# Second FFN of a two-FFN encoder layer: one low part moved from VectorE to an accumulating DMA, the first pair's preparation one block later, and the first half's output scaling one block later

## The chip, the cores and the metric

One NeuronCore of a Trainium2 chip. The metric is the device time in microseconds (us). Before the change it is 821.62 us, the median of three runs (821.60 to 821.70).

## The reference

One layer of an encoder on 512 positions of width 1024, in float32:

```python
x = x + 0.5 * swiglu(rms_norm(x, ffn1_norm), ffn1_w_gate, ffn1_w_up, ffn1_w_down)
h = rms_norm(x, mix_norm); u = h @ w_in
x = x + jnp.concatenate([fourier_mixer(...), gqa_attention(...)], axis=-1) @ w_out
x = x + 0.5 * swiglu(rms_norm(x, ffn2_norm), ffn2_w_gate, ffn2_w_up, ffn2_w_down)
return rms_norm(x, final_norm)
# swiglu(h, g, u, d) = (silu(h @ g) * (h @ u)) @ d ; hidden width 2752
```

## The kernel before, in words

Everything is kept transposed: `x[k]` (tile `gx`) holds 128 of the 1024 features by 512 positions. A float32 product is made of two rounded parts: a **high part** (a cast or copy on ScalarE, ACT below) and a **low part**, source minus high part (`lows`, L128, a subtraction on VectorE, DVE). Each 128x128 block of weights then takes three matmuls on TensorE (PE): high by high, high by low, low by high (`product`, L184). A low part can also be made without DVE: `rest_by_dma` (L157 and L158) lets ACT write minus the high part, and an accumulating DMA from GpSimd's queue (POOL) then adds the source to it.

The layer runs in three stages: the first FFN (`ffn`, tiles with 0 in the name of the norm), the mixer (a list of names sets the order), and the second FFN (`ffn` again, `n_` is 2; "stage 2" below). `ffn` treats the hidden width as 21 chunks of 128 and a tail "t" of 64 columns, in four groups. In stage 2 the groups are (0, t, 1), 2 to 7, 8 to 13 and 14 to 20.

- The first three plain chunks (0, 1, 2) and the tail are multiplied directly (`gate`, PSUM tiles `gu`), 24 matmuls of 512 columns for each 128 columns of gate or up. Meanwhile `operands` (L329) prepares the right-hand sides for the rest: for i = 0 to 3, a block `b_i` (x times gain times 1/rms, L337, 128x512 twice), four differences `t_i` (L344), the high parts (L347) of three quarters of `b_i` and of all of `t_i`, and their low parts. The low part of `t_i` (128x1024) is always DVE's; that of `b_i` (128x768) is DVE's for i = 0 and 1 and a DMA's for i = 2 and 3.
- All other chunks are made in pairs of gate and up by a scheme with seven products instead of eight (`seven`, L420, PSUM tiles `r`, `p`, `q`). Their weights come from `prepare`: two loads of 512 KB on SP's queue (`raw_g` and `raw_u`, L371), sums and differences (`s`, L394), casts (L379, L388) and low parts (L128). The steps of `prepare` are handed out one by one, between the blocks of what runs at that time.
- After each group, `down` multiplies the group's chunks by the down weights, for d = 0 to 7 (PSUM tiles `dn`, loads `raw_dn` at L152, cast at L170, low at L128), and `residual` (L544, DVE) adds the result to `x[d]`. For the first group of stage 2 a block d has 8 matmuls: 3 for chunk 0, 2 for the tail (L502, L503), 3 for chunk 1. In its order the first low weight part is used by the third matmul.

`raw_u`, `raw_dn` and the direct weights share three load buffers (tag `raw`); `raw_g` and the `b_i` share two (tag `raw_g`). A load therefore waits until an earlier user of its buffer has been read for the last time. In stage 2 the first pair is chunk 3: `prepare(3)` is called at block d = 1 of the first group's `down`, in stage 1 at d = 2.

PE and SP run in the written order. The order on ACT, DVE and POOL is chosen when the program is built, by a scheduler that knows the dependences; each engine then runs its own list in order.

The end (`closing`): for the last group, d = 5 to 7 are made by features for positions 0 to 255 and by tokens for positions 256 to 511, 128 positions at a time (c = 2 and c = 3, `by_tokens`, L534: 7 steps i = 0 to 6 of three matmuls). Between these steps stand the sums for 1/rms of the first half, `finish_half` (L1314: two transposes, L261, put the row of 1/rms into PSUM; ACT copies it to `rb`, L269; DVE scales six blocks in three instructions, L1327; POOL scales two, L1322; and each result is stored), and `finish` for c = 2 inside c = 3's steps (another L261, which needs 1/rms of c = 2). That 1/rms is made after c = 2's last matmul by a square with a sum on ACT (L1356), an addition on DVE (L1366) and a power on POOL (L1367). c = 3 goes through the same three instructions, and then through L1387 and L1391 to the last stores.

Of the kernel before, what the change touches and what calls it, by code (L numbers as in the profile page):

```python
# [86 lines left out]
def encoder(ctx, tc, A, out):  # L87
# [19 lines left out]
    def bank(name):  # L107
        return pp.tile([P, S], F32, tag="bank", name=name)
# [18 lines left out]
    def lows(lo, src, hi):  # L127
        nc.vector.tensor_tensor(out=lo, in0=src, in1=asf(hi), op=ALU.subtract)  # L128
# [26 lines left out]
    def rest_by_dma(lo, hi, src):  # L155

        nc.scalar.activation(lo, asf(hi), AF.Copy, scale=-1.0)  # L157
        nc.gpsimd.dma_start(out=lo, in_=src, accum_op=ALU.add)  # L158
# [123 lines left out]
    def ffn(norm, after, wgu, wd, wdt, groups, opening, closing):  # L282
# [4 lines left out]
        n_ = norm.n  # L287
        n_plain = len(groups[0])
        with tc.tile_pool(name=f"act{n_}", bufs=1) as ap, tc.tile_pool(name=f"sums{n_}", bufs=2) as sp:
# [7 lines left out]
            def place(j):  # L297
                where[j] = free.pop(0)
                return where[j]
# [8 lines left out]
            def gate(c, between={}, by_dma=False):  # L308
                whi, wlo = weights(wgu[c], f"gu{n_}_{c}", by_dma=by_dma)
                ps = bank(f"gu{n_}_{c}")  # L310
                for k in range(KD):
                    between.get(k, int)()
                    product(ps, whi[:, k, :], wlo[:, k, :], hh[k], hl[k], k == 0, k == KD - 1, turn=True)
                return ps

            def tail_weights():

                raw = wp.tile([P, D], F32, tag="raw", name=f"rawt{n_}")
                nc.sync.dma_start(out=raw[0:FT], in_=wdt)
                nc.sync.dma_start(out=raw[FT:P], in_=wdt)  # L320
                thi = slot()
                plain.insert(0, plain.pop())
                nc.scalar.copy(thi, raw)
                for i in range(2):
                    c = slice(i * S, (i + 1) * S)
                    wt.append(tp.tile([P, S], F32R, tag="sq", name=f"wt{n_}_{i}"))
                    nc.scalar.copy(wt[i][0:FT], asf(thi[0:FT, c]))
                    lows(wt[i][FT:P], raw[FT:P, c], thi[FT:P, c])
# [4 lines left out]
            def operands(rp, i0, i1):  # L333
                for i in range(i0, i1):
                    b = sp.tile([P, 4, HALF], F32, tag="raw_g", name=f"b{n_}_{i}")
                    for o, k in ((0, i), (2, i + KH)):
                        nc.vector.scalar_tensor_tensor(  # L337
                            out=b[:, o : o + 2].rearrange("p a b -> p (a b)"), in0=x[k],
                            scalar=gains[:, norm.n, k : k + 1], in1=rp, op0=ALU.mult, op1=ALU.mult,
                        )  # L340
                    b12, b11, b22, b21 = (b[:, o] for o in range(4))
                    t = sp.tile([P, 4, HALF], F32, tag=("s12", "s34")[i % 2], bufs=1, name=f"t{n_}_{i}")
                    for o, (p, q) in enumerate(((b12, b11), (b22, t[:, 0]), (b22, b12), (b21, t[:, 1]))):
                        nc.vector.tensor_tensor(out=t[:, o], in0=p, in1=q, op=ALU.subtract)  # L344
                    for src, c in ((b[:, 1:], slice(0, 3)), (t, slice(3, 7))):
                        h, l = rt[:, c, 0, i], rt[:, c, 1, i]
                        nc.scalar.copy(h, src)  # L347
                        if src is t or i < 2:
                            lows(l, src, h)
                        else:  # L350
                            rest_by_dma(l, h, src)

            def back(ts):
                plain[:] = [t for t in plain if all(t is not q for q in ts)]
# [188 lines left out]
            def residual(d, ps, t):  # L543
                nc.vector.scalar_tensor_tensor(  # L544
                    out=x[d][:, t], in0=ps[:, t], scalar=0.5, in1=x[d][:, t], op0=ALU.mult, op1=ALU.add
                )

            every = slice(0, S)
            for gi, group in enumerate(groups):
                last = gi == len(groups) - 1  # L550
                ahead = []
                if gi:
                    rest = seven(range(group[0] + 1, min(group[-1] + 2, NF)), ready)
                else:
                    lent = [acts[:, FRONT + i * KD * P : FRONT + (i + 1) * KD * P] for i in range(PLACES - 4, PLACES)]
                    plain.extend(lent)
                    row = []
                    pss = dict(enumerate(opening(gate, lambda: norm.column([norm.acc]), lambda: row.append(norm.row()))))
                    back(lent[:2])
                    due, parts, left = [*pss, "t"], list(range(KH)), range(2 * len(pss), 2 * n_plain)  # L560
                    pss["t"] = [gate(2 * NF)]
                    tail_weights()
                    for i, c in enumerate(left):
                        pss.setdefault(c // 2, []).append(gate(c, by_dma=i in (1,) if n_ else i > 0))
                        if due:
                            j = due.pop(0)
                            evacuate(at[:, place(j)], n_, pss[j], norm)
                        if c % 2 and c != left[-1]:
                            due.append(c // 2)
                        while len(parts) * len(left) > (len(left) - 1 - i) * KH:  # L570
                            o = parts.pop(0)
                            operands(row[0], o, o + 1)

                    def rest():
                        evacuate(at[:, place(n_plain - 1)], n_, pss[n_plain - 1], norm)

                def added(d, ps):
                    residual(d, ps, every)
                    if last:
                        (after.sums if closing else after.add)(d)  # L580
                    if ahead:
                        f, *a = ahead.pop(0)
                        f(*a)

                waiting, downs = [], []
                for d in range(KD):
                    if last and closing and d == KD - LAST:
                        closing(
                            [(e, down(e, group, gi)) for e in range(d, KD)], residual,
                            lambda ps, c: by_tokens(ps, c, group), finished,  # L590
                        )
                        break
                    if last and d == KD - 2:
                        back(lent)
                    ps = bank(f"dn{n_}_{d}_{gi}")
                    while len(downs) < min(d + 1 + (0 if gi or not n_ else 2), KD):
                        downs.append(down(len(downs), group, gi))
                    steps = downs[d](ps, every)
                    for _ in range(len(group) - (last and d < 2)):
                        next(steps)  # L600
                    waiting.append((d, ps, steps))
                    if d == (1 if gi or n_ else 2) and not last:
                        ready = prepare(groups[gi + 1][0] + 1)
                        ahead.extend(ready[1])
                    if d == 0:
                        rest()
                        if last:

                            lent = slots[KD - 2 : KD]
                            plain[2:2] = lent  # L610
                            continue
                    for d_, ps, steps in waiting:
                        for _ in steps:
                            pass
                        added(d_, ps)
                    waiting = []
                for f, *a in ahead:
                    f(*a)
                if not gi:
                    back(lent)  # L620
                free.extend(where[j] for j in group)
# [711 lines left out]
    def closing(downs, residual, by_tokens, finished):  # L1333
# [62 lines left out]
        for c in (2, 3):  # L1396
            ps = bank(f"last{c}")
            for i, _ in enumerate(by_tokens(ps, c)):
                if (c, i) == (2, 2):
                    n3.column([n3.acc], 0, 2)  # L1400
                    sums = bank("ss3_2")
                    n3.sum(sums, 2, [n3.acc])
                    n3.mean(sums, 2, 3)
                if (c, i) == (2, 5):
                    finish_half()
                if (c, i) == (3, 3):
                    finish(*done[-1])
            inverse(c, ps, z)
            done.append((c, ps))
# [126 lines left out]
```

## Time and profile before

| what | us |
|---|---|
| median of three runs | 821.62 |
| the profiled execution | 822.25 |
| its span, first to last instruction | 820.4 |
| outside of the span | 1.85 |
| direct products of stage 2 begin / its first `down` begins | 485.62 / 524.00 |
| first seven-product pair of stage 2 begins | 539.24 |
| last matmuls of c = 3 begin / span ends | 812.52 / 820.4 |

How to read it: times are from the span's start. PEld is PE's loading of the stationary operand, which runs ahead of the matmul that uses it. A row of the timeline has start, length, engine, line, operation, output<-inputs, shapes and count; in square brackets stands how long the engine had been idle and what ended that. Successive instructions overlap by about 0.1 us in these rows, so what one of them costs its engine is the distance from its start to the next one's start, a little less than its own length. Names leave buffer numbers out: which block a row belongs to follows from its place in the engine's order.

### The profile page before, as it was taken

Reading aid. Unit: us, or ns where it says so; the run is one execution under the profiler, and the core shown is the slowest. Engines: PE = TensorE matmul, PEld = TensorE weight load, DVE = VectorE, ACT = ScalarE, POOL = GpSimd, SP = SyncE. Lnnn points to the kernel's source line nnn. Section 1 sums busy time; section 2 is a strip of 40 time slices with the busy share of each in tenths; the row PEclk is TensorE's granted clock in tenths of the full one; section 3 lists DMA queues with packets and bytes.
Section 4 is the critical chain, followed back from the end, with each engine's and each line's share of the span. In section 5 each row is a group of like instructions: output and inputs, shape, how many; then the busy total and the mean of one; then the engine's idle time right before and its main releaser. Section 6 shows DMA issues by size and latency. Waiting matters only on the chain.

```text
span 820.4 us, 13609 instructions
## 1 busy us (share of the span) xinstructions
PE 813.2 (99%) x5362; PEld 745.9 (91%) x5362; DVE 638.9 (78%) x1004; ACT 482.4 (59%) x809; POOL 28.1 (3%) x30
## 2 busy tenths in 40 slices
PE   9999999999999999999999999999999999999997
PEld 7889999899989998889998888899989999899986
DVE  7898896479856847799998579998945896479574
ACT  7763674157523735699998458556632673257462
POOL 0110000000000000220000000100000000000001
PEclk9999999999999999999999999999999999999999
DMA  7664322323142213342101233552333322322222
GB/s 257 173 145 178 126 93 77 124 103 141 59 155 71 95 61 116 129 147 67 64 26 52 84 119 93 127 171 107 95 122 115 127 97 70 130 104 97 69 77 103
DMA packets 31168, 89.58 MB, mean 109 GB/s; under 512 B 3712, under 2 KB 8832, under 8 KB 31104
## 3 DMA queue, kind: packets, MB, share of 16 engines
q1 hardware_dynamic: 27776, 82.61, 29.3%
q0 software_dynamic: 2608, 5.12, 3.4%
q10 hardware_dynamic: 720, 0.98, 0.3%
q8 instruction: 42, 0.69, 0.3%
q14 instruction: 22, 0.18, 0.1%
HBM read 84.24 MB, written 2.10 MB: 105 GB/s over the span
## 4 chain that ended last, share of the span: by engine, by line
PE 93%; DVE 2%; ACT 1%; DMA 1%; issue 1%; POOL 0%; POOLq 0%; DVEq 0%; ACTq 0%
PE dn L184 25%; PE r L420 23%; PE q L420 12%; PE gu L184 7%; PE mix L184 6%; PE p L420 6%; PE gu L709 3%; PE mix L1203 2%; PE mix L1169 2%; PE mix L1007 1%; PE mix L1008 1%; PE mix L1009 1%; PE mix L1066 1%; PE mix L1143 1%; PE mix L1144 1%
## 5 line engine op out<-in xcount | busy, mean ns | idle before, releaser
L420 PE MATMUL r<-rt,ring 128*128 128x256 f32 x1686 | 209.2, 276 | 0.0
L184 PE MATMUL dn<-at,ring 128*128 128x512 f32 x900 | 203.3, 381 | 0.4 <-DVE ring L128 0.4
L420 PEld LDWEIGHTS r<-rt,ring 128*128 128x128 f32 x1686 | 200.3, 188 | 0.8
L184 PEld LDWEIGHTS dn<-at,ring 128*128 128x128 f32 x900 | 168.1, 188 | 29.8 <-DVE ring L128 1.5
L420 PE MATMUL q<-rt,ring 128*128 128x256 f32 x840 | 106.7, 276 | 0.0
L128 DVE TENSOR_TENSOR ring<-s,ring 128x1024 fp32r<-128x1024 f32 x70 | 85.7, 1224 | 24.0 <-ACT ring L379 20.6
L420 PEld LDWEIGHTS q<-rt,ring 128*128 128x128 f32 x840 | 100.4, 188 | 0.1
L544 DVE SCALAR_TENSOR_TENSOR gx<-dn,gx 128x512 f32<-128x512 f32 x61 | 42.0, 691 | 66.7 <-PE dn L184 66.7
L379 ACT CAST ring<-s 128x1024 fp32r<-128x1024 f32 x70 | 73.5, 1050 | 28.0 <-PE p L420 12.7
L170 ACT CAST ring<-raw_dn 128x768 fp32r<-128x768 f32 (+3 forms) x58 | 45.3, 784 | 70.8 <-PE dn L184 59.9
L128 DVE TENSOR_TENSOR ring<-raw_dn,ring 128x768 fp32r<-128x768 f32 (+3 forms) x58 | 51.6, 893 | 5.7 <-PE r L420 4.4
L420 PE MATMUL p<-rt,ring 128*128 128x256 f32 x420 | 53.3, 276 | 0.0
L128 DVE TENSOR_TENSOR ring<-raw_g,ring 128x1024 fp32r<-128x1024 f32 x35 | 42.8, 1222 | 11.1 <-PE p L420 10.2
L420 PEld LDWEIGHTS p<-rt,ring 128*128 128x128 f32 x420 | 50.2, 188 | 0.0
L184 PE MATMUL gu<-ring 128*128 128x512 f32 x216 | 48.9, 381 | 0.0
L379 ACT CAST ring<-raw_g 128x1024 fp32r<-128x1024 f32 x35 | 36.8, 1051 | 17.6 <-DMA raw_g<-in_wgu 11.9
L184 PEld LDWEIGHTS gu<-ring 128*128 128x128 f32 x216 | 40.4, 188 | 6.9
L428 ACT COPY p<-r 128x256 f32<-128x256 f32 x35 | 13.0, 371 | 46.7 <-PE r L420 46.3
L452 ACT ACTIVATE g<-g 128x512 f32<-128x512 f32 x35 | 22.1, 633 | 23.5 <-DVE g L451 23.3
L388 ACT CAST ring<-raw_u 128x512 fp32r<-128x512 f32 x35 | 21.8, 624 | 15.9 <-PE q L420 15.0
L465 DVE TENSOR_TENSOR u<-g,u 128x512 f32<-128x512 f32 x35 | 24.1, 690 | 6.1 <-ACT u L464 6.0
L184 PE MATMUL mix<-near,ring 128*128 128x512 f32 x120 | 28.8, 381 | 0.0
(266 smaller groups left out, 1314.5 us busy)
## 6 DMA issues: line engine op xcount, KB each, us to landing
raw_g<-in_wgu SPq DMA_DIRECT2D x35, 512.0 KB, 3.6
raw_u<-in_wgu SPq DMA_DIRECT2D x35, 512.0 KB, 4.4
raw_dn<-in_wd SPq DMA_DIRECT2D x40, 384.0 KB, 3.1
raw_gu<-in_wgu SPq DMA_DIRECT2D x12, 512.0 KB, 3.9
raw_o<-in_wo SPq DMA_DIRECT2D x8, 512.0 KB, 3.6
raw_dn<-in_wd SPq DMA_DIRECT2D x8, 448.0 KB, 3.5
raw_wq<-in_wins SPq DMA_DIRECT2D x4, 512.0 KB, 3.5
raw_f<-in_winf SPq DMA_DIRECT2D x4, 512.0 KB, 3.5
```

The lines of the kernel that those rows point to most:

```text
L128: nc.vector.tensor_tensor(out=lo, in0=src, in1=asf(hi), op=ALU.subtract)
L170: nc.scalar.copy(hi[:, :n, :], raw[:, :n, :])
L184: nc.tensor.matmul(ps, a, b, start=first and b is mhi and a is whi, stop=last and a is wlo)
L379: nc.scalar.copy(hi, src)
L388: nc.scalar.copy(hi, src)
L420: nc.tensor.matmul(ps[:, t], a[:, ks], b[:, i, t], start=first and i == 0 and o == 0, stop=i == KH - 1 and o == 2, skip_group_check=not first,
L452: nc.scalar.activation(b["g"], b["g"], AF.Silu)
L465: nc.vector.tensor_tensor(out=u, in0=b["g"], in1=u, op=ALU.mult)
L544: nc.vector.scalar_tensor_tensor(out=x[d][:, t], in0=ps[:, t], scalar=0.5, in1=x[d][:, t], op0=ALU.mult, op1=ALU.add)
L709: nc.tensor.matmul(turned(pss[c]), w[:, k % 2, c], turned(m[k]), start=k == 0 and m is hh and w is hi, stop=k == KD - 1 and w is lo,)
L1169: nc.tensor.transpose(pts[n][:, c * P : (c + 1) * P], prob[t, b, c][:, kc * P : (kc + 1) * P], ident)
L1203: nc.tensor.matmul(turned(outs[t, b]), w, turned(p), start=kc == 0 and i == 0, stop=kc == 3 and i == 1)
```

## The change

Three edits, in three places:

```diff
                     for src, c in ((b[:, 1:], slice(0, 3)), (t, slice(3, 7))):
                         h, l = rt[:, c, 0, i], rt[:, c, 1, i]
                         nc.scalar.copy(h, src)
-                        if src is t or i < 2:
+                        if src is t or i < (1 if n_ else 2):
                             lows(l, src, h)
                         else:
                             rest_by_dma(l, h, src)
...
                     waiting.append((d, ps, steps))
-                    if d == (1 if gi or n_ else 2) and not last:
+                    if d == (1 if gi else 2) and not last:
                         ready = prepare(groups[gi + 1][0] + 1)
                         ahead.extend(ready[1])
...
-                if (c, i) == (2, 5):
+                if (c, i) == (2, 6):
                     finish_half()
```

In stage 2 the low part of `b_1` is now made by ACT and a DMA, as those of `b_2` and `b_3` are. `prepare(3)` is called at d = 2. `finish_half` stands behind all seven steps of c = 2 instead of behind six.

What moves on the engines, as the built programs have it. First SP, at the loads of stage 2's first `down` and first pair (`raw_dn_3_0` is block d = 3 of group 0). Before:

```order
L152 DMA raw_dn_3_0_5340<-in_wd 128x256
L371 DMA raw_g_3_5352<-in_wgu 128x1024
L371 DMA raw_u_3_5353<-in_wgu 128x1024
L152 DMA raw_dn_4_0_5362<-in_wd 128x256
L152 DMA raw_dn_5_0_5377<-in_wd 128x256
```

and after the change:

```order
L152 DMA raw_dn_3_0_5341<-in_wd 128x256
L152 DMA raw_dn_4_0_5355<-in_wd 128x256
L371 DMA raw_g_3_5367<-in_wgu 128x1024
L371 DMA raw_u_3_5368<-in_wgu 128x1024
L152 DMA raw_dn_5_0_5377<-in_wd 128x256
```

The load for d = 4 now stands ahead of the pair's loads. With that the buffers change hands: by the waits in the programs, `raw_u_3` took the buffer of d = 1 and now takes that of d = 2; d = 5 took that of `raw_u_3` and now takes that of d = 3; d = 6 took that of d = 3 and now takes that of `raw_u_3`; d = 4 took that of d = 2 and now takes that of d = 1.

Second DVE, in the same stretch (`rt<-t_2` is a low part of `operands`, `ring<-raw_dn_3_0` the low part of block d = 3's weights, `gx<-dn_0_0` the residual of d = 0, `s_2_3` the sums of pair 3). Before:

```order
L128 TENSOR_TENSOR ring<-raw_dn_2_0_5318,ring 128x256
L128 TENSOR_TENSOR rt_5006<-t_2_5257,rt_5006 128x4x256
L128 TENSOR_TENSOR rt_5006<-t_3_5299,rt_5006 128x4x256
L629 TENSOR_TENSOR u2p<-gu_5_5271,rb_3385 128x512
L128 TENSOR_TENSOR ring<-raw_g_3_5352,ring 128x1024
L394 TENSOR_TENSOR s_2_3_5356<-raw_u_3_5353 128x512
L394 TENSOR_TENSOR s_2_3_5357<-raw_g_3_5352,raw_u_3_5353 128x512
L631 TENSOR_TENSOR u2p<-g2p,u2p 128x512
L128 TENSOR_TENSOR ring<-raw_u_3_5353,ring 128x512
L544 SCALAR_TENSOR_TENSOR gx<-dn_0_0_5309,gx 128x512
L128 TENSOR_TENSOR ring<-raw_dn_3_0_5340,ring 128x256
```

and after:

```order
L128 TENSOR_TENSOR rt_5006<-t_2_5258,rt_5006 128x4x256
L128 TENSOR_TENSOR rt_5006<-t_3_5300,rt_5006 128x4x256
L128 TENSOR_TENSOR ring<-raw_dn_2_0_5319,ring 128x256
L128 TENSOR_TENSOR ring<-raw_g_3_5367,ring 128x1024
L629 TENSOR_TENSOR u2p<-gu_5_5272,rb_3385 128x512
L631 TENSOR_TENSOR u2p<-g2p,u2p 128x512
L544 SCALAR_TENSOR_TENSOR gx<-dn_0_0_5310,gx 128x512
L128 TENSOR_TENSOR ring<-raw_dn_3_0_5341,ring 128x256
L394 TENSOR_TENSOR s_2_3_5371<-raw_u_3_5368 128x512
L394 TENSOR_TENSOR s_2_3_5372<-raw_g_3_5367,raw_u_3_5368 128x512
```

The three instructions on `raw_u_3` now stand behind the low part for d = 3, and that for d = 2 stands behind two long low parts of `operands`. Further down, the low part for d = 5 moves ahead of the last difference of pair 3 and that for d = 6 ahead of the long low part of its first sums, while one low part of 128x512 and one sum of 128x512 change places around d = 4.

Third POOL, from stage 2 to the end, as a difference (`r<-squares` is the power L1367 for c = 2 and c = 3, `gx<-gx,rb` the two scalings of `finish_half`):

```order
 L158 DMA ring<-in_wgu 128x1024
-L158 DMA rt_5006<-b_2_5254 128x3x256
-L158 DMA rt_5006<-b_3_5296 128x3x256
+L158 DMA rt_5006<-b_1_5205 128x3x256
+L158 DMA rt_5006<-b_2_5255 128x3x256
+L158 DMA rt_5006<-b_3_5297 128x3x256
 L256 TENSOR_TENSOR r_4993<-ms_4994,mhalf 128x2
+L1367 TENSOR_TENSOR r_4993<-squares,mhalf 128x1
 L1322 TENSOR_TENSOR gx<-gx,rb_4995 128x256 x2
-L1367 TENSOR_TENSOR r_4993<-squares,mhalf 128x1 x2
+L1367 TENSOR_TENSOR r_4993<-squares,mhalf 128x1
```

One more transfer is issued, and the power for c = 2 stands ahead of the two scalings. In the same way ACT's square for c = 2 (L1356) now stands ahead of the copy to `rb`, and DVE's addition (L1366) ahead of the three scalings (L1327). DVE's `b_3` (L337) now waits for `b_1`'s transfer too, since it takes that block's buffer.

## The prediction

> **What bounds the kernel now.** I read the page's busy times and its chain first, then who PE waited for, and then the places of the waits in the timeline.
>
> ```profile
> PE 813.2 (99%) x5362; PEld 745.9 (91%) x5362; DVE 638.9 (78%) x1004; ACT 482.4 (59%) x809; POOL 28.1 (3%) x30
> PE 93%; DVE 2%; ACT 1%; DMA 1%; issue 1%; POOL 0%; POOLq 0%; DVEq 0%; ACTq 0%
> PE dn L184 <- DVE ring L128: 0.4, 1, 0.4
> PE rp L261 <- POOL r L1367: 0.2, 1, 0.2
> ```
>
> PE is busy for 99% of the span and 93% of the chain is PE. The change takes no matmul away, so it can gain only what PE loses, and the two named waits of PE are exactly at the places that it touches: a low part of a down weight in stage 2, and POOL's power near the end. By these rows there would be 0.4 + 0.2 = 0.6 us to win. But matmul ends are modelled, so I take distances of starts instead.
>
> ```profile
> 524.00 0.82 PE L184 MATMUL dn<-at,ring 128*128 128x512 f32 x3
> 530.29 0.19 PEld L184 LDWEIGHTS dn<-at,ring 128*128 128x128 f32 x1 [0.82 <-DVE ring L128]
> 533.97 0.19 PEld L184 LDWEIGHTS dn<-at,ring 128*128 128x128 f32 x1 [0.27 <-DVE ring L128]
> 536.03 0.19 PEld L184 LDWEIGHTS dn<-at,ring 128*128 128x128 f32 x1 [0.44 <-DVE ring L128]
> 539.24 1.65 PE L420 MATMUL r<-rt,ring 128*128 128x256 f32 x13
> 600.62 27.72 PE dn L184 x126
> ```
>
> Undisturbed, a matmul of this kind costs 27.72 / 126 = 0.22 us (last row, a later group). The first `down` of stage 2 has 8 x 8 = 64 of them, 14.08 us, and took 539.24 - 524.00 = 15.24. So **1.16 us** are lost there, in three places: the weight loads for d = 3, 5 and 6 waited for DVE's low parts. At the end:
>
> ```profile
> 807.35 1.79 PE L534 MATMUL last<-ring,at 128*128 128x384 f32 x9
> 808.97 0.39 PE L261 MATMUL rp<-ident,r 128*128 128x128 f32 x2
> 809.95 2.25 PE L534 MATMUL last<-ring,at 128*128 128x384 f32 x12
> 812.44 0.32 PE L261 MATMUL rp<-ident,r 128*128 128x128 f32 x1 [0.24 <-POOL r L1367]
> ```
>
> Nine token matmuls take 808.97 - 807.35 = 1.62, 0.18 each; twelve from 809.95 end at 812.11, and the next instruction started at 812.44. **0.33 us** are lost.
>
> The Trainium skill ("Perfetto Trace Analysis", Identifying the Most-Contended Engine) judges PE by its weight loads, not by matmul occupancy. By the loads' idle times the first `down` would lose 0.82 + 0.27 + 0.44 = 1.53 us instead of 1.16, and the sum below would be 1.86. I keep the starts, since a load may wait while earlier matmuls still run.
>
> **The low part of `b_1`.**
>
> ```profile
> 503.51 0.96 DVE L128 TENSOR_TENSOR rt<-b,rt 128x768 fp32r<-128x768 f32 x1
> 504.38 0.42 DVE L344 TENSOR_TENSOR t<-b,t 128x256 f32<-128x256 f32 x1
> 511.02 1.40 DVE L337 SCALAR_TENSOR_TENSOR b<-gx,rp 128x512 f32<-128x512 f32 x2
> DVE ring L128 <- ACT ring L379: 0.5, 1, 0.5
> ```
>
> DVE loses one instruction worth 504.38 - 503.51 = 0.87 us. From 496 to the end of the first `down` its only wait over 0.2 us is the last row, for the cast of `raw_g`, so everything behind moves ahead by 0.87 until something else is late. ACT gets one copy (L157) of 0.84 us, and POOL one transfer:
>
> ```profile
> 502.86 1.05 ACT L170 CAST at<-raw_gu 128x1024 fp32r<-128x1024 f32 x1 [1.59 <-PE gu L184]
> 512.48 0.85 ACT L157 ACTIVATE rt<-rt 128x768 fp32r<-128x768 f32 x1
> 513.90 1.29 POOL L158 DMA_DIRECT2D rt<-b  x1 [12.12 <-ACT rt L157]
> DMA to landing us min/median/max: 4.8/5.4/6.4
> ```
>
> The copy falls into the 1.59 us in which ACT waited for PE; without that cover it would push the next cast by 0.84. POOL had been idle for 12.12 us. The new cost is a wait: `b_3` (511.02 before, 510.15 now) needs `b_1`'s buffer. The high part of `b_1` is what ACT did last before its 1.59 us of idling, so it ends at 502.86 - 1.59 = 501.27, and the copy at 502.1; with 4.8 to 6.4 us (all accumulating transfers of this kernel) it lands at 506.9 to 508.5, 1.6 us or more in time. Queued behind `b_3` on DVE are all low parts of the down weights, so this margin counts. I take nothing for it; the other end stands among the rivals. The transfer's landing at 508.5 is also 30 us ahead of the pair that reads it (539.24).
>
> The Trainium skill ("SBUF — State Buffer", the box on the "DVE blocks DMA" trap) speaks against this edit: a transfer issued from GpSimd can stand still while a DVE copy holds the port that they share; it gives 620 ns alone and 3100 ns beside one. With these 2.5 us more, an estimate by that page, the landing would be at 511.0 and DVE would lose its 0.87; the sum would fall to about 1.0. The trace does not agree: `b_2`'s transfer was issued in 1.29 us (513.90) in a stretch where DVE did not rest, though its work there is differences and no plain copies.
>
> **The pair one block later.** What moves behind, and what each low part then has as margin:
>
> ```profile
> 521.80 0.42 DVE L128 TENSOR_TENSOR ring<-raw_dn,ring 128x256 fp32r<-128x256 f32 x1
> 522.25 2.36 DVE L128 TENSOR_TENSOR rt<-t,rt 128x1024 fp32r<-128x1024 f32 x2
> 524.52 0.69 DVE L629 TENSOR_TENSOR u2p<-gu,rb 128x512 f32<-128x512 f32 x1
> 529.22 0.69 DVE L544 SCALAR_TENSOR_TENSOR gx<-dn,gx 128x512 f32<-128x512 f32 x1
> 529.82 0.42 DVE L128 TENSOR_TENSOR ring<-raw_dn,ring 128x256 fp32r<-128x256 f32 x1
> 531.36 0.42 DVE L128 TENSOR_TENSOR at<-raw_dn,at 128x256 fp32r<-128x256 f32 x1
> 533.49 0.42 DVE L128 TENSOR_TENSOR ring<-raw_dn,ring 128x256 fp32r<-128x256 f32 x1
> 535.56 0.42 DVE L128 TENSOR_TENSOR ring<-raw_dn,ring 128x256 fp32r<-128x256 f32 x1
> 536.49 0.42 DVE L128 TENSOR_TENSOR at<-raw_dn,at 128x256 fp32r<-128x256 f32 x1
> ```
>
> The five short ones from 529.82 on are d = 3 to 7. Undisturbed, block d starts at 524.00 + 1.76 d and uses its low part 0.44 later: 529.72, 531.48, 533.24, 535.00 and 536.76. The new starts are the old ones less 0.87, less what moves behind (0.60 for 128x512, by 529.82 - 529.22; 1.14 for 128x1024, half of the 2.27 between 522.25 and 524.52):
> - d = 3: three instructions on `raw_u` go behind it: 529.82 - 0.87 - 1.80 = 527.15, over 2 us in time.
> - d = 4: one goes ahead, one behind: 530.49, ends 530.91, 0.57 in time.
> - d = 5: 533.49 - 0.87 - 0.60 = 532.02, 0.80 in time.
> - d = 6: 535.56 - 0.87 - 1.14 = 533.55, 1.03 in time.
> - d = 7: the same set ahead: 535.62, 0.72 in time.
>
> A weight load has to go ahead of its matmul by about one matmul, 0.22, which leaves 0.35 at the tightest. So the 1.16 us go. What is late next is `raw_u`:
>
> ```profile
> 521.10 0.33 SPq L371 DMA_DIRECT2D raw_g<-in_wgu  x1
> 521.51 0.38 SPq L371 DMA_DIRECT2D raw_u<-in_wgu  x1
> raw_u<-in_wgu SPq DMA_DIRECT2D x35, 512.0 KB, 4.4
> raw_g<-in_wgu SPq DMA_DIRECT2D x35, 512.0 KB, 3.6
> ```
>
> It now takes the buffer of d = 2, whose low part stands behind two long ones: 521.80 - 0.87 + 2.27 = 523.20, done at 523.6. Its load then lands 3.6 to 4.4 us later, at 527.2 to 528.0, where DVE wants it at 527.5 (behind d = 3). That is a wait of 0 to 0.5 against a margin of 0.35; I take no loss, by the lower figure, since `raw_g` was loaded beside it before and now leaves about 2 us earlier. SP's one load moved ahead (d = 4, 128 KB) costs some 0.4 us of issue, and the pair's own parts are wanted only from 538 on.
>
> **The end.** The power for c = 2 no longer waits behind the two scalings:
>
> ```profile
> 809.80 1.88 DVE L1327 TENSOR_TENSOR gx<-gx,rp 128x512 f32<-128x512 f32 x3 [2.12 <-ACT rb L269]
> 809.90 0.49 ACT L1356 ACTIVATE sqt<-last 128x384 f32<-128x384 f32 x1
> 811.83 0.55 POOL L1367 TENSOR_TENSOR r<-squares,mhalf 128x1 f32<-128x1 f32 x1 [0.55 <-DVE squares L1366]
> 812.42 0.62 DVE L1376 SCALAR_TENSOR_TENSOR y<-last,r,gt 128x384 f32<-128x384 f32 x1 [0.66 <-POOL r L1367]
> 814.42 0.16 DVE L249 TENSOR_SCALAR ms<-ss 128x1 f32<-128x1 f32 x1 [0.66 <-PE ss L242]
> ```
>
> The twelve matmuls of c = 2 now run without the transposes between them, so the square starts about 0.2 earlier, at 809.7. With its 0.49, an estimated 0.4 for reading out its sum and DVE's addition, and POOL's 0.55, the power is done at some 811.15 instead of 811.83 + 0.55 = 812.38: almost 1 us ahead of the 812.11 at which PE wants it. The 0.33 us go. In exchange the copy to `rb` waits for the square, and DVE's scalings, which wait for that copy, start near 810.8 instead of 809.80. Of this 1.0 the 0.66 in which DVE waited for the power (812.42) and the addition that now stands ahead (some 0.15) are given back, so `finish` starts 0.2 later. Before, DVE was through with it at 814.42 - 0.66 = 813.76, so now at 813.96, and it is next wanted for c = 3 at 814.42 - 0.33 = 814.09: hidden, by 0.13 us. The stores of the first half (1 MB) start 1 us later and have to be gone before the last ones, which I also cost at nothing; without that cover it would be part of that 1 us.
>
> **Sum:** 1.16 + 0.33 = 1.49 us. The profiled execution, 822.25 (span 820.4 and 1.85 around it), would be 820.76. It lies 0.63 above the median 821.62; I predict for the median 821.62 - 1.49 = **820.1 us**.
>
> **The rivals.**
> - Only part of it: `raw_u` comes late, or one of d = 4 to 7 is still waited for, or the late stores stand before the last ones. Then 0.3 to 0.8 of the 1.49 stays: 820.4 to 820.9. For it: margins of 0.35 and 0.13. Against: `raw_g` no longer loads at the same time.
> - More than PE's starts show: the idle times of the weight loads at d = 3, 5 and 6 count in full (0.82 + 0.27 + 0.44 + 0.33 = 1.86 us): 819.8. For it: a matmul's end is modelled. Against: the starts, which are not.
> - It does nothing of note, since DVE's place is refilled (a wait for each of the three goes over to another block): only the end's 0.33 or less, 821.3 to 821.6. For it: DVE has little idle time to absorb anything. Against: the five margins.
> - Slower: `b_1`'s transfer comes late and holds `b_3` with every low part behind it. For it: it shares its queue with a 512 KB transfer issued just ahead of it. Against: the landing times of all eight such transfers. Up to a landing at 510.5 (510.15 and the margin of 0.35) nothing happens; from there each us costs PE one. For slower than before it has to land after 512, for 0.2% slower after 513.6, 11.5 us after its issue, where the longest took 6.4; at 512.5 to 515 the time would be 822.1 to 824.6. It is the one wait that the change adds ahead of the low parts.
>
> **How the numbers follow.** The full sum, 48%; part of it, 22%; more, 14%; nothing of note, 6%; slower, 10%. 0.2% is 1.64 us, about what a measurement of this kernel tells from no change. The full sum is just below it, so faster by more than that takes the second rival and some of the full sum's scatter: 22%. Slower 10%, within 68%. The range reaches from 819.6 (the loads' figure and 0.2 of scatter) to 821.4, which leaves out the slower case and a part of the nothing case.
>
> **What would show it.** In the profile after: from the first `down`'s start to the first `r`, 14.1 us instead of 15.2, and no weight load waiting for DVE there; the single L261 without a wait for POOL; L158 three times in stage 2, and no wait of DVE for a DMA at L337. A DVE wait at the first L394 of the pair means the first rival. I am wrong if PE waits at a place where it did not before, or if the last stores start later relative to PE's end.

## The result and the profile after

| | before, us | after, us | ratio, 95% interval |
|---|---|---|---|
| medians of 22 runs each | 821.77 | 820.70 | 0.9986 (0.9980 to 0.9992) |
| span of the profiled execution | 820.4 | 818.9 | |
| stage 2's first `down`, first start to first `r` | 15.24 | 14.37 | |
| from the first L526 to the last nine L534 (c = 2 and the single L261) | 7.63 | 7.28 | |

The kernel is 1.07 us faster, inside the 0.2% that the prediction called no change. It had put 1.49 us on two places. In the experiments below some runs of a kernel lie about 2 us above its others (9 of 35 and 11 of 29 runs of the kernel before on two of the chips, none in the table above), so a median there can shift with their number. Busy times and chain of the page after:

```profile
PE 812.4 (99%) x5362; PEld 746.1 (91%) x5362; DVE 637.5 (78%) x1003; ACT 483.1 (59%) x810; POOL 29.3 (4%) x31
PE 95%; DVE 2%; ACT 1%; POOL 1%; issue 1%; DMA 0%; POOLq 0%; DVEq 0%; ACTq 0%
```

DVE has one instruction less, ACT and POOL one more, and PE's share of the chain rose from 93% to 95%. The first `down`, PE and its weight loads (timeline; start, length, engine, line; in brackets the idle time and what ended it):

```profile
523.80 0.82 PE L184 MATMUL dn<-at,ring 128*128 128x512 f32 x3
531.45 0.19 PEld L184 LDWEIGHTS dn<-at 128*128 128x128 f32 x1 [0.42 <-DVE at L128]
538.17 1.65 PE L420 MATMUL r<-rt,ring 128*128 128x256 f32 x13
```

538.17 - 523.80 = 14.37 for the 14.08 of 64 matmuls. One weight load still waits, that of d = 4, and 0.29 us are lost there; 0.87 of the 1.16 are gone. DVE in the same stretch:

```profile
524.57 1.22 DVE L128 TENSOR_TENSOR ring<-raw_g,ring 128x1024 fp32r<-128x1024 f32 x1 [1.14 <-ACT ring L379]
525.71 0.68 DVE L629 TENSOR_TENSOR u2p<-gu,rb 128x512 f32<-128x512 f32 x1
527.64 0.42 DVE L128 TENSOR_TENSOR ring<-raw_dn,ring 128x256 fp32r<-128x256 f32 x1
527.97 0.68 DVE L394 TENSOR_TENSOR s<-raw_u 128x512 f32<-128x512 f32 x1
530.98 0.42 DVE L128 TENSOR_TENSOR at<-raw_dn,at 128x256 fp32r<-128x256 f32 x1
```

The first row is `raw_g`'s low part: DVE now stands 1.14 us for the cast of `raw_g`, where it stood 0.46 before. The second is L629, which stood ahead of that wait and now stands behind; the next instruction starts at 526.43, 0.72 later. The third is d = 3's low part, at 3.84 from the first `down`'s start, and the fourth, on `raw_u`, had no wait. The last is d = 4's low part, at 7.18 from the first `down`'s start. What leads to that cast, on SP, ACT, POOL and DVE (one row from each engine's timeline, then ACT's copy and the cast behind it):

```profile
519.35 0.33 SPq L371 DMA_DIRECT2D raw_g<-in_wgu  x1
523.49 1.05 ACT L379 CAST ring<-raw_g 128x1024 fp32r<-128x1024 f32 x1 [1.15 <-DMA raw_g<-in_wgu]
501.10 0.85 ACT L157 ACTIVATE rt<-rt 128x768 fp32r<-128x768 f32 x1
502.66 1.05 ACT L170 CAST at<-raw_gu 128x1024 fp32r<-128x1024 f32 x1 [0.71 <-PE gu L184]
502.52 1.29 POOL L158 DMA_DIRECT2D rt<-b  x1 [0.95 <-DVE t L344]
509.96 1.40 DVE L337 SCALAR_TENSOR_TENSOR b<-gx,rp 128x512 f32<-128x512 f32 x2
```

`raw_g`'s load was issued at 519.35 (before: 521.10), and its cast waited 1.15 us for it. The copy for `b_1` (501.10) left ACT 0.71 us of idling ahead of the next cast, POOL's issue took 1.29, and `b_3` (509.96) waited for nothing: `b_1`'s transfer landed 5.4 us after its issue, at 507.9, 2.0 us in time. The end, PE, DVE and POOL:

```profile
808.78 2.33 PE L534 MATMUL last<-ring,at 128*128 128x384 f32 x12
810.95 0.27 PE L261 MATMUL rp<-ident,r 128*128 128x128 f32 x1
809.13 0.16 DVE L1366 TENSOR_TENSOR squares<-squares,ms 128x1 f32<-128x1 f32 x1 [2.64 <-ACT sqt L1356]
812.88 0.16 DVE L249 TENSOR_SCALAR ms<-ss 128x1 f32<-128x1 f32 x1 [0.35 <-PE ss L242]
809.37 0.55 POOL L1367 TENSOR_TENSOR r<-squares,mhalf 128x1 f32<-128x1 f32 x1 [2.30 <-DVE squares L1366]
```

The single L261 starts 2.17 after twelve matmuls' start, which is 12 x 0.18, without a wait; the power (POOL's row) was done at 809.92, 1.03 us early.

### The profile page after: what moved, and what is told of

Its sections match the earlier page's. It is cut to its first block, busy times and chain, and to the rows that moved or that the text cites. A ratio compares the mean times of both kernels' runs of the same rounds, so it can differ in the third digit from the quotient of the medians.

```text
span 818.9 us, 13611 instructions
## 1 busy us (share of the span) xinstructions
PE 812.4 (99%) x5362; PEld 746.1 (91%) x5362; DVE 637.5 (78%) x1003; ACT 483.1 (59%) x810; POOL 29.3 (4%) x31
## 4 chain that ended last, share of the span: by engine, by line
PE 95%; DVE 2%; ACT 1%; POOL 1%; issue 1%; DMA 0%; POOLq 0%; DVEq 0%; ACTq 0%
PE dn L184 25%; PE r L420 23%; PE q L420 12%; PE gu L184 8%; PE mix L184 6%; PE p L420 6%; PE gu L709 3%; PE mix L1203 2%; PE mix L1169 2%; PE mix L1007 1%; PE mix L1008 1%; PE mix L1009 1%; PE mix L1066 1%; PE mix L1143 1%; PE mix L1144 1%
## 5 line engine op out<-in xcount | busy, mean ns | idle before, releaser
L428 ACT COPY p<-r 128x256 f32<-128x256 f32 x35 | 12.9, 369 | 44.9 <-PE r L420 44.6
```

## The experiments

**The theories.** A: DVE runs its list in order, and in this stretch it stands at a cast or a landing of the first pair's loads; what it saves ahead of that point is lost there, and what stands behind the point decides whether PE waits. B: DVE's amount of work is late, so the gain is the 0.87 us of work taken away. C: the later preparation alone makes the gain. "First down" is the distance from the first `down`'s first matmul to the first `r`; 14.08 would be no loss.

First the three edits apart. All four ran on one chip, where the kernel before had a median of 822.46.

**e1_low_by_dma**, edit 1 alone:

```diff
-                        if src is t or i < 2:
+                        if src is t or i < (1 if n_ else 2):
```

> Only the first edit: the low part of b_1 by ACT and a transfer; pair 3 is still prepared at d = 1. Theory A (the pair's loads and casts pace DVE: what DVE saves ahead of raw_g's cast it spends waiting for that cast, and what counts for PE is which low parts stand behind the pair's sums): the first down of stage 2 keeps most of its loss, 14.8 to 15.1 us from its first matmul to the first r instead of 15.24 before and 14.37 after, with DVE waiting 0.8 us or more for raw_g's cast; the time falls by 0.1 to 0.4. Rival B (the gain is the 0.87 us that DVE saves, the order adds nothing): 14.4 us or less, and 0.8 us off the time. The end as before: PE waits for the power of c = 2.

Ratio 0.9996 (0.9985 to 1.0006), first down 538.69 - 523.89 = 14.80. DVE and the weight loads:

```profile
524.23 1.23 DVE L128 TENSOR_TENSOR ring<-raw_g,ring 128x1024 fp32r<-128x1024 f32 x1 [0.72 <-ACT ring L379]
533.66 0.19 PEld L184 LDWEIGHTS dn<-at,ring 128*128 128x128 f32 x1 [0.77 <-DVE ring L128]
537.26 0.19 PEld L184 LDWEIGHTS dn<-at 128*128 128x128 f32 x1 [0.20 <-DVE at L128]
```

0.87 us less work gained 0.44 of PE's time against the profile of before, and DVE's wait at the cast grew from 0.46 to 0.72, a little less than A's 0.8. By these two profiles half is missing for B. But in this program too L629 stands behind the cast, a second profile of the old first `down` (15.57, with e3_half_later) would make the gain 0.77, and the interval of the time holds both forecasts. So this run leans to A and does not settle it.

**e2_pair_later**, edit 2 alone:

```diff
-                    if d == (1 if gi or n_ else 2) and not last:
+                    if d == (1 if gi else 2) and not last:
```

> Only the second edit: pair 3 prepared at d = 2. As built, DVE's and ACT's orders are those of before; only one load changes its place on SP. Theory A: first down 15.1 to 15.4 us, no change in the time (within 0.2 us). Rival C (the later preparation alone clears the way for the low parts): 14.4 us or less, and 0.8 us off the time.

Ratio 1.0006 (0.9993 to 1.0019), first down 539.44 - 523.77 = 15.67.

```profile
525.31 1.23 DVE L128 TENSOR_TENSOR ring<-raw_g,ring 128x1024 fp32r<-128x1024 f32 x1 [0.34 <-ACT ring L379]
527.00 0.69 DVE L394 TENSOR_TENSOR s<-raw_u 128x512 f32<-128x512 f32 x1 [0.46 <-DMA raw_u<-in_wgu]
```

Only SP's order differs from before here. `raw_u` is loaded later, and DVE, with its old list, stands a second time, 0.46 us for its landing. C falls.

**e3_half_later**, edit 3 alone:

```diff
-                if (c, i) == (2, 5):
+                if (c, i) == (2, 6):
```

> Only the third edit: finish_half one block later. Both theories: first down as before (15.2 us); the single L261 for c = 2 follows its matmuls at once; 0.33 us off the time. If the later stores collide with the last ones, the distance from the last token matmuls to the span's end grows by what is lost.

Ratio 0.9990 (0.9981 to 0.9999).

```profile
525.60 1.23 DVE L128 TENSOR_TENSOR ring<-raw_g,ring 128x1024 fp32r<-128x1024 f32 x1 [0.78 <-ACT ring L379]
812.13 0.27 PE L261 MATMUL rp<-ident,r 128*128 128x128 f32 x1
```

The single L261 has no wait, and from the first L526 (804.88) to the last L534 (812.16) it took 7.28 instead of 7.63: the whole gain of the end by itself. The first row is a second look at the old first `down`: with the same program the wait at the cast was 0.78 instead of 0.46, and first down 539.17 - 523.60 = 15.57 instead of 15.24. So one profile of this stage is good to some 0.3 us at best.

**e12_no_end**, edits 1 and 2 without 3:

> The first two edits together, without the third. First down as after the change, 14.3 to 14.4 us, with one wait of a weight load, at d = 4. The end as before. The time falls by 0.8 to 0.9 us. If A holds, this is more than the sum of the two edits alone; by B it equals the first edit alone, by C the second alone.

Ratio 0.9985 (0.9975 to 0.9994), first down 538.20 - 523.66 = 14.54.

```profile
531.46 0.19 PEld L184 LDWEIGHTS dn<-at 128*128 128x128 f32 x1 [0.57 <-DVE at L128]
811.31 0.32 PE L261 MATMUL rp<-ident,r 128*128 128x128 f32 x1 [0.24 <-POOL r L1367]
```

Edit 2, worth nothing alone, seems to help together with edit 1: 14.80 becomes 14.54, which is within the scatter of one profile, and the median 822.29 becomes 821.35, while the two intervals of the ratio overlap. The first `down` missed its 14.3 to 14.4: DVE also waited 0.19 us for `raw_u`. The end keeps its old wait of 0.24.

Next, with the whole change, the suspected wait was made longer or moved. These four ran on another chip (before: 822.01).

**after_again**, the changed kernel once more:

> The changed kernel once more, beside the next three. Both theories: 0.7 to 1.4 us below the kernel before; the first down of stage 2 (64 matmuls and what they wait for) 14.3 to 14.7 us, with one wait left on DVE's low part for d=4, of 0.3 to 0.6 us.

820.79 us, ratio 0.9985 (0.9976 to 0.9994). First down 538.80 - 524.08 = 14.72, not 14.37, and the wait at d = 4 is longer than the 0.3 to 0.6 expected:

```profile
528.59 0.69 DVE L394 TENSOR_TENSOR s<-raw_u 128x512 f32<-128x512 f32 x1 [0.27 <-DMA raw_u<-in_wgu]
531.61 0.42 DVE L128 TENSOR_TENSOR at<-raw_dn,at 128x256 fp32r<-128x256 f32 x1
532.08 0.19 PEld L184 LDWEIGHTS dn<-at 128*128 128x128 f32 x1 [0.77 <-DVE at L128]
```

The wait at `raw_g`'s cast is the same 1.14, but now DVE also waits 0.27 us for `raw_u`'s landing, and d = 4's low part comes at 531.61 - 524.08 = 7.53.

**x_g_twice**, an extra 128 KB load ahead of `raw_g`'s, so that the latter is issued at 521.20:

```diff
+                    if n_ and j == 3 and t is g:
+                        nc.sync.dma_start(out=t.rearrange("p (a b) -> p a b", b=P)[:, :2], in_=wgu[c][:, :2])
                     nc.sync.dma_start(out=t.rearrange("p (a b) -> p a b", b=P), in_=wgu[c])
```

> The changed kernel with an extra load of the first quarter of raw_g ahead of its load, in stage 2's first pair alone, so that raw_g's load starts some 2 to 3 us later; nothing else is done. A: raw_g's cast comes that much later, DVE's wait ahead of raw_g's low part grows from 1.14 us to 3 to 4, each us of it shows in the first down: 16 to 17.5 us, the kernel 1.5 to 3 us over the changed one. B: the first down stays within 0.3 us of 14.4, since raw_g's parts are wanted only behind it.

822.19 us, ratio 1.0006 (0.9997 to 1.0015); the median is 1.40 over after_again's. First down 538.89 - 523.28 = 15.61.

```profile
526.00 1.23 DVE L128 TENSOR_TENSOR ring<-raw_g,ring 128x1024 fp32r<-128x1024 f32 x1 [1.83 <-ACT ring L381]
531.68 0.42 DVE L128 TENSOR_TENSOR at<-raw_dn,at 128x256 fp32r<-128x256 f32 x1
532.16 0.19 PEld L184 LDWEIGHTS dn<-at 128*128 128x128 f32 x1 [1.61 <-DVE at L128]
```

DVE's work is the changed kernel's, only later loaded and with a few neighbours exchanged (L629 stands ahead of the cast again), and PE loses 1.24 us more than in the first profile, 0.47 more than in the longest of the three profiles of the changed kernel; the intervals of the time do not overlap. B falls. The cost was less than A's 1.5 to 3 us: `raw_g` was issued 1.6 to 1.9 us later instead of 2 to 3, and DVE did L629, with 0.57 of waiting for PE ahead of it, before it came to stand 1.83 us at the cast.

**x_dma0**, the low part of `b_0` by transfer too, 0.87 us less work for DVE:

```diff
-                        if src is t or i < (1 if n_ else 2):
+                        if src is t or i < (0 if n_ else 2):
```

> The changed kernel with b_0's low part by transfer as well, so DVE has 0.87 us less to do in the stage. A (DVE stands still at raw_g's cast, whenever it gets there): the wait ahead of raw_g's low part grows by 0.5 to 0.9 us to 1.6 to 2.0, the first down stays at 14.3 to 14.7 us, the kernel within 0.2 us of the changed one, or slower where a third transfer beside b_2's and b_3's makes raw_g's load later. B (DVE's work is what is late): the wait stays near 1.1, the last wait at d=4 goes, first down 14.1, the kernel 0.2 to 0.3 us under the changed one.

823.43 us, ratio 1.0021 (1.0012 to 1.0029); the median is 2.64 over after_again's. First down 540.28 - 523.14 = 17.14.

```profile
501.07 2.60 POOL L158 DMA_DIRECT2D rt<-b  x2 [0.15 <-DVE t L344]
507.33 1.41 DVE L337 SCALAR_TENSOR_TENSOR b<-gx,rp 128x512 f32<-128x512 f32 x2 [2.12 <-DMA rt<-b]
524.55 1.23 DVE L128 TENSOR_TENSOR ring<-raw_g,ring 128x1024 fp32r<-128x1024 f32 x1 [0.45 <-ACT ring L379]
527.64 0.69 DVE L394 TENSOR_TENSOR s<-raw_u 128x512 f32<-128x512 f32 x1 [0.54 <-DMA raw_u<-in_wgu]
530.66 0.42 DVE L128 TENSOR_TENSOR ring<-raw_dn,ring 128x256 fp32r<-128x256 f32 x1
531.13 0.19 PEld L184 LDWEIGHTS dn<-at,ring 128*128 128x128 f32 x1 [2.15 <-DVE ring L128]
```

Both expectations missed it. The wait at the cast did not grow but fell to 0.45: DVE now stood earlier, 2.12 us at `b_2` (507.33), whose buffer is `b_0`'s and is still being read by the transfer. With that `raw_g`'s low part came 0.64 us later (1.41 from the first `down` instead of 0.77). The low part for d = 3 (530.66) came much later than that, 7.52 from the first `down` instead of 3.84, and PE waited 1.72 for it: in this program three sums of the pair and `raw_u`'s low part, 0.60 each, and a wait of 0.54 for `raw_u`'s landing stand ahead of it, where the changed kernel has them behind. So the edit changed DVE's order too, and by these rows most of the loss is the order's. The wait for the transfer itself is the prediction's slower rival, one block ahead of where it was looked for: a transfer issued right behind a 512 KB one, and 4.1 us later DVE comes for the buffer (507.33 - 2.12 = 505.21).

**x_d3**, the first pair prepared at d = 3:

```diff
-                    if d == (1 if gi else 2) and not last:
+                    if d == (1 if gi else 3 if n_ else 2) and not last:
```

> The changed kernel with the first pair of stage 2 prepared one more block further on, at d=3: DVE's low part of raw_g then stands behind d=3's low part and behind two additions to gx, so DVE is not held ahead of them until raw_g's cast is done. A (DVE's order stands still at raw_g's cast): the wait ahead of raw_g's low part falls from 1.14 us to under 0.2, d=3 to d=5 are in time, d=6 or d=7 may wait 0 to 0.3; first down 14.1 to 14.4 us, the kernel 0 to 0.3 us under the changed one. B (what is left is DVE's work, whose sum stays): the wait for d=4 stays or moves to d=6 or d=7 with 0.3 to 0.5 us, first down 14.3 to 14.6, the kernel within 0.2 of the changed one; if the first r of the pair is late, PE waits at L420 behind the first down and the kernel is 0.3 or more slower.

Ratio 1.0001 (0.9992 to 1.0009); the median, 821.59, is 0.80 over after_again's, and the profiled run, 824.05, is the longest of its 11. First down 538.64 - 523.87 = 14.77.

```profile
523.95 0.38 SPq L371 DMA_DIRECT2D raw_g<-in_wgu  x1
529.55 1.22 DVE L128 TENSOR_TENSOR ring<-raw_g,ring 128x1024 fp32r<-128x1024 f32 x1 [1.27 <-ACT ring L379]
535.44 0.19 PEld L184 LDWEIGHTS dn<-at,ring 128*128 128x128 f32 x1 [0.78 <-DVE ring L128]
544.77 1.68 PE L420 MATMUL q<-rt,ring 128*128 128x256 f32 x12 [0.40 <-ACT p L428]
546.29 2.99 PE L420 MATMUL r<-rt,ring 128*128 128x256 f32 x24
```

A's numbers failed, as the edit moved the loads with the list: on SP they now stand behind one more `raw_dn`, so `raw_g` was issued at 523.95, and DVE stood 1.27 at its cast again, six instructions further on. The wait went over to d = 6. In the first pair PE then waited 0.40 for ACT's copy `p` (L428), which stands on ACT behind casts for the second pair; one of these waited for a late sum on DVE and began at 542.88, in the changed kernel at 541.46.

That wait is the smaller part of what this profile lost there. The matmuls of the pairs behind it were slower too. The last row above has 24 of them; in the changed kernel the same block is

```profile
545.10 2.88 PE L420 MATMUL r<-rt,ring 128*128 128x256 f32 x24
```

By starts, twelve took 1.41 us instead of 1.36, at the same granted clock of 1.00, until the next `down`. From the first `r` to that `down` it is 597.17 - 538.64 = 58.53 us, against 55.89 in the profile after, in after_third and in y_o12: 2.64 more, of which the idle time is 0.40. What sets the slower pace is open.

Last, DVE's order alone, with every load and cast where the changed kernel has it (before, on this chip: 822.57).

**after_third**, the changed kernel:

> The changed kernel beside the next two, for a comparison on the same chip: first down 14.3 to 14.8 us, 0.7 to 1.4 us below the kernel before.

821.66 us, ratio 0.9989 (0.9978 to 1.0000). First down 538.97 - 523.83 = 15.14, over the 14.8 expected: at the cast DVE waited 1.18, and for `raw_u`

```profile
528.76 0.69 DVE L394 TENSOR_TENSOR s<-raw_u 128x512 f32<-128x512 f32 x1 [0.66 <-DMA raw_u<-in_wgu]
531.78 0.41 DVE L128 TENSOR_TENSOR at<-raw_dn,at 128x256 fp32r<-128x256 f32 x1
532.24 0.19 PEld L184 LDWEIGHTS dn<-at 128*128 128x128 f32 x1 [1.19 <-DVE at L128]
```

0.66 us. `raw_u`'s load, issued 0.34 to 0.36 us ahead of the first `down` in the three profiles of this kernel, took 4.1, 4.8 and 5.3 us to land.

**y_o13**, DVE in the written order for d = 1 to 3 (the low part of `raw_g` behind that for d = 4):

```diff
+                scope = None
                 for d in range(KD):
+                    if n_ and not gi and d == 1:
+                        scope = tc.manual_schedule(engines={mybir.EngineType.PE, mybir.EngineType.SP, mybir.EngineType.DVE})
+                        scope.__enter__()
+                    if scope and d == 4:
+                        scope.__exit__(None, None, None)
+                        scope = None
```

> The changed kernel with the same loads and casts in the same order, but DVE's instructions of the blocks d = 1 to 3 of stage 2's first down in the written order: the low part of raw_g then stands behind the low part for d = 4 instead of ahead of that for d = 3, and two of the pair's four sums move behind d = 5 and d = 6. DVE's work is the same. A (DVE's order holds it at a cast whose load is late): no wait for raw_g's cast, one for raw_u's landing of 0.3 to 0.8 us, all of d = 3 to d = 7 in time, first down 14.1 to 14.2 us, the kernel 0.2 to 0.4 us under the changed one. B (DVE's work in the stretch is what is late): a wait of the weight loads stays, at d = 5 or later, first down 14.3 to 14.7, the kernel within 0.2 us of the changed one. A cost elsewhere: the low part of the pair's first sums is made some 2 us later, and the third block of the first pair could wait for it.

Ratio 0.9993 (0.9981 to 1.0004), while the median, 823.08, is 0.51 over that of before, so the time decides nothing here. The profiled run, 823.89, is the longest of its 12. First down 538.40 - 523.66 = 14.74.

```profile
528.48 0.69 DVE L394 TENSOR_TENSOR s<-raw_g,raw_u 128x512 f32<-128x512 f32 x1 [1.83 <-DMA raw_u<-in_wgu]
531.36 0.19 PEld L184 LDWEIGHTS dn<-at 128*128 128x128 f32 x1 [0.47 <-DVE at L128]
533.43 0.19 PEld L184 LDWEIGHTS dn<-at,ring 128*128 128x128 f32 x1 [0.43 <-DVE ring L128]
544.61 1.68 PE L420 MATMUL q<-rt,ring 128*128 128x256 f32 x12 [0.47 <-ACT p L428]
546.13 2.99 PE L420 MATMUL r<-rt,ring 128*128 128x256 f32 x24
```

The wait at `raw_g`'s cast is gone, and the whole of it came back at `raw_u`'s landing: 1.83 us, more than twice what A expected, since `raw_u` took 5.1 us to land and DVE came there 1.2 us earlier (2.99 after the first `down`'s start, 4.17 to 4.27 in the changed kernel). PE still waited at d = 4 and d = 5, so A's 14.1 to 14.2 failed and B's figure was nearer. Inside the first pair PE waited 0.47 as in x_d3, again for the copy behind casts of the second pair (here from 542.72 on), which is not the cost that the expectation named. The slower pace followed here too: 597.01 - 538.40 = 58.61 us to the next `down`. These are the only two profiles of the case with a wait inside that pair, and the only two with that pace in it.

**y_o12**, the same for d = 1 and 2 alone (the scope ends at d = 3):

```diff
-                    if scope and d == 4:
+                    if scope and d == 3:
```

> As the one before, but with the written order for d = 1 and d = 2 alone: raw_g's low part also stands behind the low part for d = 4, and three of the pair's sums and raw_u's low part stand ahead of it. A: DVE gains the wait for raw_g's cast, but now stands at raw_u's landing for 0.6 to 1.2 us ahead of the low part for d = 4, which comes at 7.2 to 7.6 us from the first down's start: first down 14.3 to 14.8 us, the kernel within 0.3 us of the changed one. B: the same work, so the same 14.3 to 14.7; only the comparison with the kernel before it tells them apart.

Ratio 0.9998 (0.9989 to 1.0008). First down 539.73 - 523.78 = 15.95.

```profile
527.71 0.69 DVE L394 TENSOR_TENSOR s<-raw_u 128x512 f32<-128x512 f32 x1 [0.94 <-DMA raw_u<-in_wgu]
531.79 0.19 PEld L184 LDWEIGHTS dn<-at 128*128 128x128 f32 x1 [0.77 <-DVE at L128]
533.86 0.19 PEld L184 LDWEIGHTS dn<-at,ring 128*128 128x128 f32 x1 [0.45 <-DVE ring L128]
536.52 0.19 PEld L184 LDWEIGHTS dn<-at,ring 128*128 128x128 f32 x1 [1.02 <-DVE ring L128]
```

The same instructions as y_o13 with the same loads, 0.89 us less waiting for `raw_u`, and 1.21 us more lost by PE, because sums stand ahead of the low parts for d = 4 to d = 6. Neither theory gave more than 14.8. By these two profiles it is not the amount of work and not one wait alone: it is what the list holds between the landing and each low part.

## Why the prediction came out as it did

The time lay inside the range, but not as the full sum: of its cases, the one that came true is the first rival, "only part of it", which had 22%. Its own signs were mixed: PE waits at d = 4, where it did not before, which it had named as a sign of being wrong, while the sign for the first rival, a DVE wait at the pair's first L394, is missing in the profile after and came only in later ones. Point by point:

- **The end, 0.33 us: right.** 0.35 by the whole change and by edit 3 alone. The cover held: DVE had 0.35 us to spare ahead of its instruction for c = 3 (812.88), where 0.13 had been worked out, and from the last L534 to the end of the span it took 818.9 - 810.98 = 7.92, before 7.88, so the later stores met nothing.
- **`b_1`'s transfer at no cost: right**, with the cover on ACT down to 0.71 us. The Trainium skill ("SBUF — State Buffer", the box on the "DVE blocks DMA" trap) gives its rule for a two-port mode of DVE, which a float32 copy triggers. Beside this issue DVE ran only `TENSOR_TENSOR`, and the issue took 1.29 us, so no run here shows the page's case. That a late transfer can hold DVE x_dma0 shows.
- **The first `down`, 1.16 us: mis-sized**, 0.87 by the profile after. The step that failed is "so everything behind moves ahead by 0.87 until something else is late". As far as `raw_g`'s low part it was true: that starts 0.77 after the first `down` instead of 1.67, 0.90 earlier. But L629 (0.72 to the next start) had moved from ahead of that wait to behind it; the order rows of the change showed it, and the sum left it out. So the head start went into a wait of 1.14 instead of 0.46, and d = 4's low part, forecast at 530.49, 6.49 from the first `down`, came at 7.18. A landing 0.7 us sooner would have saved it too: `raw_g` took 4.1 us where it had taken 3.4. Why is open: the transfer for `b_3` was still moving in the first 0.9 us of that load, but so it was in e1_low_by_dma and e2_pair_later, where the load took 3.6 and 3.4. What L629 cost is read from the rows; no run moved it alone. The margin was sized well: 6.49 and the 0.35 left make 6.84, and the table below finds 6.89.
- **`raw_u` as "what is late next", a wait of 0 to 0.5: nearly right.** 0, 0.27 and 0.66 in three profiles of the same kernel. The sum put it at no loss; with the margin used up by L629, each of these came on top.

With these three profiles, e12_no_end (the same code in this stretch) and x_g_twice the loss can be read as a line:

| profile | wait, `raw_g` | wait, `raw_u` | low part d = 4 at | lost in first down | idle of that load |
|---|---|---|---|---|---|
| after | 1.14 | 0 | 7.18 | 0.29 | 0.42 |
| e12_no_end | 1.01 | 0.19 | 7.33 | 0.46 | 0.57 |
| after_again | 1.14 | 0.27 | 7.53 | 0.64 | 0.77 |
| after_third | 1.18 | 0.66 | 7.95 | 1.06 | 1.19 |
| x_g_twice | 1.83 | 0 | 8.40 | 1.53 | 1.61 |

The low part's start less what was lost is 6.87 to 6.89 in all five: past 6.89 us each us of DVE is a us of PE, whichever load made it. The last column is why starts were the right measure: the idle time of the load is 0.08 to 0.13 more than what PE lost. The Trainium skill ("Perfetto Trace Analysis", Identifying the Most-Contended Engine) judges PE by the busy share of its weight loads; that is 91% before and after and does not show this change.

The sum also took one profile of each for the kernel. Over the profiles here the first `down` lost 1.16 and 1.49 with the old code (before, e3_half_later), mean 1.33, and 0.29, 0.46, 0.64 and 1.06 with the new, mean 0.61. The gain is then 0.71, with the end's 0.35 about 1.1; the medians say 1.07, 1.22 and 0.91 in the three comparisons. No kernel tried here is measurably faster than the changed one. What makes `raw_u` land after 4.1 us in one execution and 5.3 in another stays open.

## What to carry to other kernels

Work taken off an in-order engine helps the instructions behind it only as far as the next wait for a load. Walk the new list from the freed place to the instruction that the bounding engine needs, with every landing on the way and every instruction that has changed sides of a wait, because one that leaves the idle time ahead of a wait to stand behind it costs its full length. And where a margin is a few tenths of a us, look at more than one profile of the kernel before: landing times of one load differ by more than that.

## What was not expected of the hardware

- The same 512 KB load, issued at the same place of the same program, landed after 4.1, 4.8 and 5.3 us.
- Two accumulating transfers of 384 KB, issued one behind the other and directly behind one of 512 KB on the same queue (x_dma0, from 501.07 on), landed 6.2 and 7.1 us after their issue; the longest in the kernel before took 6.4. The next writer of `b_0`'s buffer started at 507.33.
- In both profiles in which PE waited inside the first pair (x_d3, 0.40 us, and y_o13, 0.47), the matmuls behind the wait went on at 1.41 us per twelve instead of 1.36 until the next `down`, and the stretch took 2.64 and 2.72 us longer. Two profiles do not show that the wait is the cause.
